# Two transformer blocks on one core: half-array products as alternating runs, rotation by VectorE across bands, second layer's modulation gathered by VectorE, first norm's modulation block by block

## The chip, the cores and the metric

The kernel runs on one core of a Trainium2 chip. TensorE (PE; its weight loads are listed as PEld) multiplies, VectorE (DVE), ScalarE (ACT) and GpSimd (POOL) work on tensors in the on-chip memory, and SyncE (SP) issues the loads. The metric is the device time of one execution in microseconds; a kernel's time is the median of several.

## The reference, cut to what matters

Two blocks follow each other on 256 tokens of width 1024, all in float32. The first has two layers; the second, which starts with a recurrence over the tokens, has one.

```python
def first_block(x, c, ctx, c_ctx, w_ada, ...):
    for l in range(2):
        mod_x = silu(c) @ w_ada[l] + b_ada[l]        # 9 vectors of 1024
        mod_c = silu(c_ctx) @ w_ada[l] + b_ada[l]
        h  = h  + 0.5 * g1  * swiglu(rms_norm(h)  * (1 + sc1)  + sh1)    # width 2816
        hc = hc + 0.5 * cg1 * swiglu(rms_norm(hc) * (1 + csc1) + csh1)
        p, pc = u @ w_in[l], uc @ w_in[l]             # u, uc: normed and modulated
        q_g, k_g = rms_norm(q_g), rms_norm(k_g)
        q_w, k_w, q_g, k_g = (rope(t, cos, sin) for t in (q_w, k_w, q_g, k_g))
        h = h + gm * (attention of three kinds @ w_out[l])
        ...                                           # hc likewise, then a second feed-forward
def _rope(x, cos, sin):                               # per head of 64
    x1, x2 = x[..., :32], x[..., 32:]
    return concatenate([x1 * cos - x2 * sin, x2 * cos + x1 * sin])
```

The second block's recurrence, per head of 64: `state = state * w + sa * b + v * k`, with `sa = state @ -kk`, and the output `state @ r`.

## The kernel before

**How it is tiled.** Channels lie on the 128 partitions in eight blocks (KB = 8), tokens along the free axis: columns 0 to 255 are x and 256 to 511 the context, so that one product of 512 columns serves both. Products of weights are in three parts: a weight tile of 1 MiB is loaded, ScalarE casts it (`whi`), VectorE forms the residue (`wlo`), both 128x1024 twice (`wtile`, L775), and each activation likewise has a cast and a residue (`split`, L813); `mm3` (L797) issues hi x hi, hi x lo and lo x hi.

**What sets the order.** The program is recorded as a list (class Plan, L388), and `schedule` (L514) lays it out by list scheduling: each engine takes the first recorded operation whose inputs are ready, with costs from `cost` (L472), within a window of 3000 operations and the memory that is free. The memory is 22 pages of 128x2048, a small area, three weight slots and eight banks. The result is one fixed order for each engine. Every instruction is emitted from one line (L739, in `emit`), so the trace knows tiles only as page, bank, small and w. `nc.run` (class Run, L374) records several products as one operation that nothing comes between.

**The modulation.** `ada_steps(l, g)` (L880) computes 2048 columns of `silu(c) @ w_ada`, for c and c_ctx at once: `cs` holds both vectors, padded to 32 columns, as the stationary side, and the loaded chunk of 128 rows x 2048 columns streams through four column groups of the array, 32 columns of the array each (`tile_position=(0, 32j)`), plain fp32. Eight chunks accumulate in a bank; `fin` (L912) turns the result around with small products and adds the bias. Group 0 of layer 0 holds the shift and scale of the first norm, and its eight chunks of 1 MiB come first in the program (`setup`, L835). The other groups are lists of steps that the feed-forward layers pop, one after each block (`pop_fill`, L819). Layer 1 is popped in `ffn(0, 2)`, the second feed-forward of layer 0: five groups, the last with 1024 columns, two chunks to a step. `pos_steps` (L1332), a table lookup on VectorE that the second block needs, is popped after it.

**The first feed-forward.** `norm` (L990) with `scaled` takes x and ctx already multiplied by their reciprocal norms and applies gain and shift; `ffn` (L1019) runs its first two blocks (`gate_up`, L1057) in halves, x's 256 columns first, and the other nine of each half with 512.

**The rotation.** In `finish` (L1150), for seven of 13 projections a layer, the projection is copied out of its bank, a product with a permutation matrix `perm` swaps the 32-row bands, and VectorE forms `t * cos + swapped * sin`.

**The half-array products.** In `rwkv_chunks` (L1632, called once for each of two groups of four heads) the products of `bt` and `kt` with `KR` use 64 rows of the array, one head; `TK` and the first part of `pY` fill 64 columns of it.

## Time and profile before

| | |
|---|---|
| time, median of 3 runs (lowest to highest) | 2390.52 us (2389.61 to 2391.29) |
| the profiled execution: time, span | 2394.02 us, 2392.2 us |
| mean granted clock of TensorE | 0.991 |
| PE, PEld, DVE, ACT, POOL busy | 2343.3, 2024.9, 1342.4, 973.4, 52.2 us |
| loaded | 325.00 MB, 136 GB/s over the span |

How to read it: the span runs from the first instruction to the last of one profiled execution, and times in the trace count from its start. "Busy" is the time in which an engine had at least one instruction under way. A product in plain fp32 shows as two records, one of the three-part kind as one.

### The profile page before, as it was taken

What the parts mean: (1) busy time and instruction counts of PE and PEld (TensorE: products, weight loads), DVE (VectorE), ACT (ScalarE), POOL (GpSimd) and SP (SyncE); (2) the same over time, 40 slices, a digit from 0 to 9 for tenths busy, and PEclk for the clock granted to TensorE, in tenths of its full rate; (3) what the DMA queues carried; (4) which work ended last, traced back from release to release, by engine and by line L of the source; (5) the groups of instructions that cost most, each with busy time, mean ns of one, the idle gap of its engine ahead of it and who ended that gap; (6) DMA issues with size and microseconds to landing.
All of it is one profiled execution on the core that took longest, in us unless ns stands there. A gap on an engine that the chain in (4) does not pass through costs nothing. (4 is left out here: it accounts for less than half of the span.)

```text
span 2392.2 us, 35707 instructions
## 1 busy us (share of the span) xinstructions
PE 2343.3 (98%) x14614; PEld 2024.9 (85%) x14614; DVE 1342.4 (56%) x2539; ACT 973.4 (41%) x1760; POOL 52.2 (2%) x64
## 2 busy tenths in 40 slices
PE   6999999999999999999999999999999999999998
PEld 4777788978787777888878889889999898999998
DVE  4322333585753597345333247866557677667874
ACT  4221223476632212233213235755456224646653
POOL 0000000000000000000000000000000000000000
PEclk8999999999999999999999999999999999999999
DMA  8646422212345573233123233134545110454543
GB/s 338 236 172 220 165 83 96 94 37 97 106 183 194 193 288 123 76 104 122 61 89 132 78 108 103 63 113 172 196 156 178 43 49 34 158 177 158 210 158 127
DMA packets 55041, 328.34 MB, mean 137 GB/s; under 512 B 7133, under 2 KB 10205, under 8 KB 24798
## 3 DMA queue, kind: packets, MB, share of 16 engines
q1 hardware_dynamic: 54878, 326.07, 38.2%
q8 instruction: 114, 1.87, 0.3%
q14 instruction: 49, 0.40, 0.0%
HBM read 325.00 MB, written 1.05 MB: 136 GB/s over the span
## 5 line engine op out<-in xcount | busy, mean ns | idle before, releaser
L739 PE MATMUL bank<-page,page 128*128 128x256 f32 (+5 forms) x13206 | 2233.9, 344 | 29.6 <-DMA page<-in_w_ada_dram 14.0
L739 PEld LDWEIGHTS bank<-page,page 128*128 128x128 f32 (+2 forms) x13206 | 1875.3, 186 | 318.6 <-issue 61.4
L739 ACT CAST page<-w 128x1024 fp32r<-128x1024 f32 (+2 forms) x511 | 488.7, 961 | 1000.0 <-PE bank L739 958.1
L739 DVE TENSOR_TENSOR page<-w,page 128x1024 fp32r<-128x1024 f32 (+2 forms) x511 | 567.5, 1113 | 541.6 <-ACT page L739 400.4
L739 DVE TENSOR_TENSOR page<-page,bank 128x512 f32<-128x512 f32 (+2 forms) x170 | 94.2, 569 | 242.9 <-PE bank L739 239.6
L739 DVE SCALAR_TENSOR_TENSOR page<-bank,small,page 128x256 f32<-128x256 f32 (+2 forms) x240 | 111.5, 484 | 98.3 <-PE bank L739 94.8
L739 PE MATMUL bank<-page 128*128 128x256 f32 (+9 forms) x564 | 141.1, 315 | 1.7 <-DVE page L739 1.6
L739 DVE TENSOR_TENSOR page<-page,page 128x256 fp32r<-128x256 f32 (+3 forms) x272 | 129.1, 490 | 15.2 <-ACT page L739 14.6
L739 ACT ACTIVATE page<-bank,small 128x256 f32<-128x256 f32 (+2 forms) x216 | 115.3, 546 | 33.4 <-DVE small L739 21.7
L739 ACT CAST page<-page 128x256 fp32r<-128x256 f32 (+1 forms) x167 | 78.2, 481 | 113.9 <-DVE page L739 111.9
L739 PEld LDWEIGHTS bank<-small,page 128*128 128x128 f32 x776 | 95.0, 167 | 25.3 <-ACT page L739 8.1
L739 ACT COPY page<-bank 128x512 f32<-128x512 f32 (+3 forms) x175 | 81.1, 497 | 85.8 <-PE bank L739 84.1
L739 PE MATMUL bank<-small,page 128*128 128x128 f32 (+4 forms) x776 | 108.2, 266 | 7.2 <-ACT page L739 4.5
L739 ACT ACTIVATE page<-bank 128x512 f32<-128x512 f32 (+3 forms) x168 | 84.2, 508 | 59.3 <-PE bank L739 58.5
L739 ACT ACTIVATE page<-page 128x256 f32<-128x256 f32 (+3 forms) x180 | 77.9, 446 | 67.1 <-DVE page L739 58.2
L739 PEld LDWEIGHTS bank<-page 128*128 128x128 f32 (+2 forms) x564 | 93.8, 190 | 9.1 <-DVE page L739 2.6
L739 DVE TENSOR_TENSOR page<-bank,page 128x256 f32<-128x256 f32 (+2 forms) x123 | 57.5, 488 | 39.8 <-PE bank L739 23.8
L739 POOL TENSOR_TENSOR small<-small 128x2 f32<-128x2 f32 (+2 forms) x32 | 38.2, 1196 | 1871.2 <-DVE small L739 1492.4
L739 DVE TENSOR_REDUCE small<-bank 128x1 f32<-128x512 f32 (+3 forms) x132 | 67.2, 526 | 3.6 <-PE bank L739 3.4
L739 ACT ACTIVATE page<-page,small 128x256 fp32r<-128x256 f32 (+1 forms) x124 | 56.9, 506 | 29.1 <-DVE page L739 28.6
L739 DVE COPY_PREDICATED page<-page,small 128x384 f32<-128x384 uint32 x124 | 64.8, 588 | 0.9
L739 DVE TENSOR_SCALAR page<-page,small 128x256 f32<-128x256 f32 (+2 forms) x136 | 53.7, 407 | 2.2 <-ACT page L739 1.1
(47 smaller groups left out, 384.9 us busy)
## 6 DMA issues: line engine op xcount, KB each, us to landing
w<-in_gu_dram SPq DMA_DIRECT2D x88, 1024.0 KB, 4.9
page<-in_w_ada_dram SPq DMA_DIRECT2D x64, 1024.0 KB, 7.4
w<-in_dn_dram SPq DMA_DIRECT2D x64, 704.0 KB, 4.1
w<-in_w_up_dram SPq DMA_DIRECT2D x22, 1024.0 KB, 4.8
w<-in_w_qk_dram SPq DMA_DIRECT2D x12, 1024.0 KB, 4.9
w<-in_w_gate_dram SPq DMA_DIRECT2D x12, 1024.0 KB, 4.9
w<-in_w_dn_dram SPq DMA_DIRECT2D x16, 704.0 KB, 4.0
page<-in_w_ada_dram SPq DMA_DIRECT2D x16, 512.0 KB, 4.6
```

The source lines that it names most:

```text
L739: getattr(getattr(self.real, eng), m_)(*a_, **k_)
```

## The change

It does five things.

- Layer 1's modulation no longer goes through TensorE chunk by chunk (`ada_steps_v`). VectorE keeps two accumulators of 128x2048, one each for c and c_ctx, and adds each chunk times its per-partition scalar (ScalarE makes the first one by a copy with a scale). At the end of a group two products per column group, with a stationary side `pick` that is all ones in one column, sum over the partitions; the ending (`ada_fin`) is the old one. A step is one chunk now, 45 steps instead of 25, and the loop that emptied the list behind `ffn(0, 2)` goes, so that what is left runs on into `ffn(1, 1)`.
- The first norm's group is laid out anew in memory (`w_ada0`): chunk k holds all 1024 rows of the shift and scale of channel block k. `first_mod` handles one chunk with eight 256-column products, two small products to turn it around, and the additions; `ffn` then scales block k of x and ctx and issues its products for the first two gate/up blocks, both halves in one, before it goes to block k + 1. The context and the small constants are loaded ahead of the chunks.
- The rotation's product goes: four operations of 32 rows read a band and write the swapped one, times a sine table whose signs are arranged for that; the cosine part and the sum follow.
- The 64-row products alternate between the two halves of the rows, in runs of four and with a bank for each half; `TK` and the first products of `pY` are runs as well.
- The planner holds back 5120 instead of 6144 columns of memory.

```diff
+    def first_mod(self, k, raw):
+        ps = self.aux_ps("ada")
+        with nc.run(cost=1100.0):
+            for i in range(2):
+                for j in range(4):
+                    b = 4 * i + j
+                    nc.tensor.matmul(ps[32 * j:32 * j + 32, :256], self.cs[:, b, :], raw[:, 256 * b:256 * b + 256],
+                                     start=i == 0, stop=i == 1, skip_group_check=True, tile_position=(0, 32 * j))
+        t = self.t("adat", [256])
+        nc.vector.tensor_copy(t, ps[:, :256])
+        pt = self.aux_ps("adaT")
+        for m in range(2):
+            nc.tensor.matmul(pt[:, 2 * m:2 * m + 2], t[:, P * m:P * m + P], self.rsum, start=True, stop=True)
...
+    def ada_steps_v(self, l, g):
...
+                for r in range(2):
+                    acc = st["acc"][r][:, :n]
+                    if k == 0:
+                        nc.scalar.activation(acc, raw[:, :n], AF.Copy, scale=self.cs[:, k, r:r + 1])
+                    else:
+                        nc.vector.scalar_tensor_tensor(acc, raw[:, :n], self.cs[:, k, r:r + 1], acc,
+                                                       op0=OP.mult, op1=OP.add)
...
+                for r in range(2):
+                    for j in range(nj):
+                        nc.tensor.matmul(ps[32 * j:32 * j + 32, :], self.pick[:, r],
+                                         st["acc"][r][:, 512 * j:512 * j + 512], start=r == 0, stop=r == 1,
+                                         skip_group_check=True, tile_position=(0, 32 * j))
...
+        elif scaled:
+            u = [self.blk(f"u{k}") for k in range(KB)]
+            first = [[self.mm_ps("pg"), self.mm_ps("pu")] for _ in range(ahead)]
+            for k in range(KB):
+                self.first_mod(k, raws[k])
...
+                for j in range(ahead):
+                    for i in range(2):
+                        self.mm3(first[j][i], w0[j], (i * KB + k) * P, u[k], both[0], k == 0, k == KB - 1)
...
-                    nc.scalar.activation(t, ps[:, :N], AF.Copy, scale=sc)
-                pr = self.aux_ps("rot")
-                nc.tensor.matmul(pr[:, :S], perm, t[:, :S], start=True, stop=True)
+                    x_ = ps
+                    if N > S:
+                        nc.scalar.activation(t[:, S:], ps[:, S:N], AF.Copy, scale=sc)
                 t1, t2 = self.t("rp1", [S]), self.t("rp2", [S])
-                nc.vector.tensor_tensor(t1, t[:, :S], cosT, op=OP.mult)
-                nc.vector.tensor_tensor(t2, pr[:, :S], sinT, op=OP.mult)
+                for r in range(0, P, 32):
+                    a_, b_ = slice(r, r + 32), slice(r ^ 32, (r ^ 32) + 32)
+                    nc.vector.scalar_tensor_tensor(t2[b_], x_[a_, :S], sc, sinT[a_], op0=OP.mult, op1=OP.mult)
+                nc.vector.scalar_tensor_tensor(t1, x_[:, :S], sc, cosT, op0=OP.mult, op1=OP.mult)
                 nc.vector.tensor_tensor(t[:, :S], t1, t2, op=OP.add)
...
         for g in range(5):
-            self.fill += self.ada_steps(1, g)
+            self.fill += self.ada_steps_v(1, g)
         self.ffn(0, 2)
-        while self.fill:
-            self.pop_fill()
...
+                pss = [self.aux_ps("pw") for _ in range(2)]
+                with nc.run(cost=2 * 450.0):
+                    for i, st in enumerate((bt, kt)):
+                        for s in range(2):
+                            hs = slice(64 * s, 64 * s + 64)
+                            nc.tensor.matmul(pss[s][:, S * i:S * i + S], st[hs, pr, P * tb:P * tb + P], KR[pr][hs, tb],
+                                             start=True, stop=True)
```

**How the order moves, at three places.** The first is the start of TensorE's order, before (32x512 are the chunks of the first modulation, 128x1 the sums of squares, 128x128 the spreading of the reciprocal norms, 128x256 from row 12 on the first feed-forward):

```order
L739 MATMUL bank0_67<-page1_78,page0_75 32x512 x4
L739 MATMUL bank0_67<-page4_86,page0_75 32x512 x4
L739 MATMUL bank1_68<-small_63,page0_75 128x1 x4
L739 MATMUL bank0_67<-page5_88,page0_75 32x512 x4
L739 MATMUL bank0_67<-page6_90,page0_75 32x512 x4
L739 MATMUL bank2_69<-small_63 128x128 x2
L739 MATMUL bank0_67<-page7_95,page0_75 32x512 x4
L739 MATMUL bank0_67<-page8_97,page0_75 32x512 x4
L739 MATMUL bank0_67<-page9_102,page0_75 32x512 x4
L739 MATMUL bank0_67<-page10_104,page0_75 32x512 x4
L739 MATMUL bank3_70<-small_63,page4_86 128x8 x4
L739 MATMUL bank4_71<-page6_198,page3_84 128x256
```

and now (32x256 are a chunk, 128x2 its small products, 128x512 the feed-forward):

```order
L740 MATMUL bank0_67<-small_63,page0_75 128x1 x4
L740 MATMUL bank1_68<-small_63 128x128 x2
L740 MATMUL bank2_69<-page4_88,page0_75 32x256 x8
L740 MATMUL bank3_70<-small_63,page0_75 128x1 x4
L740 MATMUL bank4_71<-small_63,page4_88 128x2 x2
L740 MATMUL bank5_72<-small_63 128x128 x2
L740 MATMUL bank6_73<-page5_98,page0_75 32x256 x8
L740 MATMUL bank7_74<-page6_101,page0_75 32x256 x8
L740 MATMUL bank0_67<-small_63,page16_210 128x2 x2
L740 MATMUL bank1_68<-small_63,page16_210 128x2 x2
L740 MATMUL bank3_70<-page17_229,page14_181 128x512
L740 MATMUL bank2_69<-page17_229,page14_181 128x512
```

Three chunks instead of eight stand ahead of the first product of the feed-forward, and both norms' sums instead of one norm's.

The second is VectorE's order in `ffn(0, 2)`, over two gate/up blocks, before (128x1024 are weight residues, the 128x512 that read a bank the gating products, the other 128x512 residues of their results):

```order
L739 TENSOR_TENSOR page10_256<-w2_66,page5_194 128x1024
L739 TENSOR_TENSOR page0_75<-page0_75,bank3_70 128x512
L739 TENSOR_TENSOR page17_414<-w2_66,page6_198 128x1024
L739 TENSOR_TENSOR page16_294<-page0_75,page16_294 128x512
L739 TENSOR_TENSOR page7_201<-w0_64,page8_206 128x1024
L739 TENSOR_TENSOR page0_75<-page0_75,bank2_69 128x512
L739 TENSOR_TENSOR page18_535<-w0_64,page5_194 128x1024
L739 TENSOR_TENSOR page17_414<-page0_75,page17_414 128x512
L739 TENSOR_TENSOR page10_256<-w1_65,page5_194 128x1024
L739 TENSOR_TENSOR page0_75<-page0_75,bank6_73 128x512
```

and now (the multiply-adds of the modulation are the operations of 128x2048):

```order
L740 SCALAR_TENSOR_TENSOR page14_3911<-page5_98,page0_75,page14_3911 128x2048
L740 SCALAR_TENSOR_TENSOR page16_210<-page5_98,page0_75,page16_210 128x2048
L740 TENSOR_TENSOR page4_506<-w0_64,page2_84 128x1024
L740 SCALAR_TENSOR_TENSOR page14_3911<-page10_3921,page0_75,page14_3911 128x2048
L740 TENSOR_TENSOR page0_75<-page0_75,bank4_71 128x512
L740 TENSOR_TENSOR page6_3625<-w0_64,page2_84 128x1024
L740 TENSOR_TENSOR page20_263<-page0_75,page20_263 128x512
L740 SCALAR_TENSOR_TENSOR page16_210<-page10_3921,page0_75,page16_210 128x2048
L740 SCALAR_TENSOR_TENSOR page14_3911<-page13_3960,page0_75,page14_3911 128x2048
L740 TENSOR_TENSOR page19_257<-w1_65,page6_3625 128x1024
L740 SCALAR_TENSOR_TENSOR page16_210<-page13_3960,page0_75,page16_210 128x2048
L740 TENSOR_TENSOR page0_75<-page0_75,bank6_73 128x512
```

Two or three multiply-adds of 128x2048 stand between the operations of a block, in which there was nothing but the layer's own work.

The third is TensorE's order at the 64-row products of the recurrence, before (a row of two is one head's):

```order
L739 MATMUL bank2_69<-page8_10489,page9_13239 128x256 x2
L739 MATMUL bank3_70<-page8_10489,page9_13239 128x256 x2
L739 MATMUL bank0_67<-page9_13239 128x256 x2
L739 MATMUL bank2_69<-page9_13239 128x256 x2
L739 MATMUL bank3_70<-page8_10489,page9_13239 128x256 x2
L739 MATMUL bank0_67<-page8_10489,page9_13239 128x256 x2
L739 MATMUL bank2_69<-page9_13239 128x256 x2
L739 MATMUL bank3_70<-page9_13239 128x256 x2
```

and now, for the second of the four runs of such a chunk (banks 2 and 6), with the products around it (dense ones in bank 1 and others in bank 3):

```order
L740 MATMUL bank1_68<-page13_7542,page4_7271 128x256 x2
L740 MATMUL bank1_68<-page13_7542,page5_5142 128x256
L740 MATMUL bank2_69<-page11_5865,page3_86 128x256
L740 MATMUL bank6_73<-page11_5865,page3_86 128x256
L740 MATMUL bank2_69<-page11_5865,page7_13219 128x256
L740 MATMUL bank6_73<-page11_5865,page7_13219 128x256
L740 MATMUL bank3_70<-page7_13219,page11_5865 128x64 x2
L740 MATMUL bank1_68<-page13_7542,page4_7271 128x256 x2
L740 MATMUL bank1_68<-page13_7542,page5_5142 128x256
L740 MATMUL bank1_68<-page2_84,page4_7271 128x256 x2
L740 MATMUL bank1_68<-page2_84,page5_5142 128x256
```

The heads alternate by bank, and dense products of another part stand between one run and the next.

## Rows read from the trace of the kernel before

**Rows 1.** The page's first part: engine, busy us (share of the span) x instructions

```profile
PE 2343.3 (98%) x14614; PEld 2024.9 (85%) x14614; DVE 1342.4 (56%) x2539; ACT 973.4 (41%) x1760; POOL 52.2 (2%) x64
```

**Rows 2.** Windows: us, busy (count) by engine, PEclk, DMA, GB/s; last row sums 625 to 1400

```profile
0.00:60.00 60.00, 41.39 (x264) 29.83 (x265) 28.02 (x68) 24.30 (x55) 5.69 (x16) 0.89 0.83 337
...
850.00:940.00 90.00, 90.00 (x436) 66.17 (x437) 85.24 (x159) 20.11 (x25) 0.00 (x0) 1.00 0.60 214
...
sum 775.00, PE 770.31 PEld 622.25 DVE 369.95 ACT 222.57 POOL 9.86; mean PE 110.04 PEld 88.89 DVE 52.85 ACT 31.80 POOL 1.41
```

**Rows 3.** Groups by shape, PE, whole span: busy, mean ns of one, idle before

```profile
L739 PE MATMUL bank<-page,page 128*128 128x512 f32 x4855 | 1150.0, 392 | 3.7 <-DVE page L739 3.4 <-ACT page L739 0.3
L739 PE MATMUL bank<-page,page 128*128 128x256 f32 x6371 | 844.9, 288 | 10.6 <-ACT page L739 6.9 <-DVE page L739 3.5
...
L739 PE MATMUL bank<-page,page 64*128 64x256 f32 x64 | 13.3, 397 | 0.0
...
L739 PE MATMUL bank<-small,page 128*128 128x2 f32 x72 | 8.6, 243 | 0.5 <-ACT page L739 0.5
```

**Rows 4.** Groups by shape, PE, 625 to 960 us: the 32-row products

```profile
L739 PE MATMUL bank<-page,page 128*32 128x512 f32 x288 | 35.0, 599 | 0.0
```

**Rows 5.** Timeline of the weight loads, 707 to 714: start, length, [wait before]

```profile
707.03 1.77 PEld L739 LDWEIGHTS bank<-page,page 128*128 128x128 f32 x8
...
711.02 1.01 PEld L739 LDWEIGHTS bank<-page,page 128*128 128x128 f32 x5 [0.84 <-ACT page L739]
```

**Rows 6.** Groups by shape, DVE, 625 to 1400 us

```profile
L739 DVE TENSOR_TENSOR page<-w,page 128x1024 fp32r<-128x1024 f32 x92 | 112.4, 1223 | 144.4 <-ACT page L739 119.8 <-PE bank L739 18.6 <-issue 3.5
L739 DVE COPY_PREDICATED page<-page,small 128x384 f32<-128x384 uint32 x124 | 64.8, 588 | 0.9
...
L739 DVE SCALAR_TENSOR_TENSOR page<-bank,small,page 128x256 f32<-128x256 f32 x66 | 29.1, 479 | 36.2 <-PE bank L739 36.0
L739 DVE TENSOR_TENSOR page<-page,page 128x512 fp32r<-128x512 f32 x40 | 27.5, 687 | 6.2 <-ACT page L739 6.2
```

**Rows 7.** Groups by shape, ACT, 625 to 1400 us

```profile
L739 ACT CAST page<-w 128x1024 fp32r<-128x1024 f32 x92 | 96.7, 1051 | 303.1 <-PE bank L739 303.1
...
L739 ACT CAST page<-page 128x512 fp32r<-128x512 f32 x40 | 24.8, 621 | 49.3 <-DVE page L739 49.3
```

**Rows 8.** Timeline of PE at 479 us, a rotation's product and what follows

```profile
479.53 0.60 PE L739 MATMUL bank<-page 128*128 128x256 f32 x2
479.78 2.41 PE L739 MATMUL bank<-page,page 128*128 128x512 f32 x9
```

**Rows 9.** Timeline of PE and its weight loads, 1865 to 1873: half-array products

```profile
1865.84 1.14 PE L739 MATMUL bank<-page,page 64*128 64x256 f32 x8
1866.81 1.92 PE L739 MATMUL bank<-page 64*128 64x256 f32 x7
...
1872.40 0.42 PEld L739 LDWEIGHTS bank<-small,page 128*128 128x128 f32 x4 [0.54 <-DVE page L739]
```

**Rows 10.** Timeline of PE, its loads and DVE, 0 to 75 us

```profile
10.25 3.08 DVE L739 TENSOR_TENSOR page<-page 128x256 f32<-128x256 f32 x6 [10.25 <-ACT page L739]
...
20.49 2.74 DVE L739 TENSOR_TENSOR page<-page,bank 128x256 f32<-128x256 f32 x8 [4.56 <-PE bank L739]
...
33.77 0.80 PE L739 MATMUL bank<-page,page 128*128 128x256 f32 x2 [1.48 <-ACT page L739]
...
66.93 8.26 PEld L739 LDWEIGHTS bank<-page,page 128*128 128x128 f32 x37 [0.84 <-ACT page L739]
```

**Rows 11.** Window 34 to 40 us, as rows 2

```profile
34.00:40.00 6.00, 3.71 (x16) 3.41 (x17) 6.00 (x14) 5.08 (x13) 0.00 (x0) 0.50 1.02 417
```

**Rows 12.** Timeline of DVE, 466 to 484 us

```profile
468.70 1.38 DVE L739 SCALAR_TENSOR_TENSOR page<-page,page 64x512 fp32r<-64x512 f32 x2
...
479.15 0.41 DVE L739 TENSOR_TENSOR page<-page,page 128x256 f32<-128x256 f32 x1
...
479.48 0.42 DVE L739 TENSOR_TENSOR page<-page 128x256 f32<-128x256 f32 x1
```

More of the change, by code (lines that the diff above doesn't have):

```diff
@@ L1027, in ffn, with glu @@
         ahead = 2
+        def glu(j, ps, sl):
+            m = sl.stop - sl.start
+            sg, hf = self.t("sg", [m]), self.t("hf", [m])
+            nc.scalar.activation(sg, ps[0][:, sl], AF.Silu)
+            nc.vector.tensor_tensor(hf, sg, ps[1][:, sl], op=OP.mult)
+            self.split(H[j], sl, hf)
         if one:
@@ L1047, in ffn @@
                 self.split(H[j], slice(0, S), h)
-        elif w0 is None:
+        elif scaled:
[3 more added lines that the diff above has]
+                self.first_mod(k, raws[k])
+                for r in halves:
+                    t, G, sh = scaled[r][k], self.G[l][0][:, k, r:r + 1], self.mod[l][:, k, r:r + 1]
+                    if r:
+                        nc.scalar.activation(t, t, AF.Identity, scale=G, bias=sh)
+                    else:
+                        nc.vector.tensor_scalar(t, t, G, sh, op0=OP.mult, op1=OP.add)
+                    self.split(u[k], parts[r], t)
+                for j in range(ahead):
+                    for i in range(2):
+                        self.mm3(first[j][i], w0[j], (i * KB + k) * P, u[k], both[0], k == 0, k == KB - 1)
+            for j in range(ahead):
+                glu(j, first[j], both[0])
+                self.pop_fill()
+        else:
             w0 = [self.wtile(self.a[f"gu{n}"][l, j]) for j in range(ahead)]
-        u = self.norm(l, i_n, halves, scaled, rb if one else None)
+        if not scaled:
+            u = self.norm(l, i_n, halves, rb if one else None)
         hg = self.hg[l][n - 1]
```

181 lines of the change are left out of this document (97 added, 84 removed).

## Prediction

> **What bounds the kernel now.** I read the page's first part first: TensorE is busy for 2343.3 of 2392.2 us [rows 1]. Only 49 us of the span are without a product, and the table by stages puts 18.6 of them into the first 60 us, where the products wait for data [rows 2]; from 850 to 940 us TensorE is busy 90.0 of 90 us while VectorE, too, is busy 85.2. So almost everywhere a microsecond of product that is taken off TensorE is a microsecond of time, as long as nobody becomes late; work for VectorE and ScalarE is free where they have room. The groups of products by shape give the prices [rows 3]: a 512-column product costs 1150.0 / 4855 = 0.237 us of TensorE, a 256-column one 844.9 / 6371 = 0.133 us. Their mean of 392 and 288 ns is latency, which overlaps.
>
> **Second layer's modulation.** Before, 36 groups of four 32-row products (two records each) take 35.0 us of TensorE between 625 and 960 us, 0.97 us a group [rows 4]. After, VectorE sums over the eight row blocks, and TensorE only spreads two sums per column group: 8 groups for the four full steps and one group's worth for the half one, 9 x 0.97 = 8.8 us. That is 26.2 us less. Each visit has a cost of its own besides: ordinary weight loads stop at 707.03 + 1.77 = 708.80 and resume at 711.02, 2.22 us for two groups of 0.97 [rows 5], so 0.2 to 0.3 us a visit, and 15 of 20 visits go: 3 us. I take 28 us, bounds 24 and 30.
> The sums cost VectorE 56 multiply-adds of 2048 elements and 14 of 1024. The longest there are today are additions: 1.22 us for 1024 elements, 0.69 for 512, so 1.04 ns an element and 0.15 fixed; a 256-element multiply-add (0.48, from a bank) is 0.06 above that line [rows 6]. So 2.35 and 1.28 us: 56 x 2.35 + 14 x 1.28 = 150 us. ScalarE gets eight copies of 2048 and two of 1024, on its own line of 1.05 and 0.62 us [rows 7]: 17 us, in a stage where it is the idlest.
> What hides the 150 us: from 625 to 1400 us VectorE is busy 370 of 775 [rows 2]; 520 of some 747 is 70%. The peak of before is the table lookup for the positions, 124 predicated copies, 64.8 us [rows 6]; the new order puts most of it behind the multiply-adds, into the next feed-forward layer, where there was room. The densest place of the new order is the one quoted: in four consecutive gate/up blocks VectorE has three, three, four and two multiply-adds plus the block's two weight residues, one gating product and one residue (3.8 us), about 10.9, 10.9, 12 and 9 us, against 48 products x 0.237 = 11.4 us for a block. That fits with little over, and weights are split about one block ahead. I charge 2 us for places where one multiply-add stands ahead of something wanted; bounds 0 and 10. If this cover were gone, one exposed multiply-add costs 2.35 us.
>
> **Rotation.** Fourteen matrix products of 256 columns in plain fp32 leave TensorE. One is at 479.53: its two passes end 0.60 us later, and the next product is drawn 0.25 us after it [rows 8], which are the two bounds; the half-array products of the same width take 13.3 us for 32, 0.42 each [rows 3]. I take 14 x 0.42 = 6 us, bounds 3.4 and 8.4. VectorE gets four 32-row operations for one of 128 rows, some 1.5 us more a rotation, 21 us, in stretches where it is half idle. ScalarE's copy becomes half as wide or goes.
>
> **Half-array products.** In the recurrence's preparation, 32 products use one half of the array's rows. The trace shows that halves can run together: the first four take from 1865.84 to 1866.81, 0.97 us, but all 16 of that chunk last until 1872.40, 6.56 us [rows 9], because the later ones wait for VectorE to empty a bank (0.54 us at the end, and the order shows three banks in turn). Four runs at 0.97 us would take 3.9 us, so at most 2.7 us a chunk, 5.3 for both. The new runs are apart and enter and leave the half-array mode each by itself, which costs some tenths like the visits above. The other two groups were next to each other already or gain an alternation here and there. I take 4 us, bounds 0 and 6.
>
> **First norm, block by block.** Before, the first product stands at 33.77 us, behind the eight chunks, and runs at half clock at first (the granted clock is 0.50, the lower of its levels, from 34 to 40); the first two blocks with the first four chunks of the next modulation are done when ordinary weight loads resume at 66.93 [rows 10, 11]. After, the loads are x, ctx, chunk 0, weights 0, chunks 1 and 2, weights 1, and so on; at 417 GB/s [rows 11] one of 1 MiB takes 2.5 us. But now the vector work stands first. From the first addition to the last scaled block of x took from 10.25 to 23.2 us [rows 10]; it starts 2.5 us earlier, and ahead of the first product there are also eight scalings of ctx (2.7 us), two weight residues (2.4), and the copies, additions and residues of chunk 0 (2.3): some 28 us, 6 us earlier than now. Behind it stand five chunk runs that were in front (5 us) and two small products more for each block (14 x 0.24 = 3.4 us [rows 3]); the two blocks go as 96 products of 512 columns at 0.237 instead of 192 of 256 at 0.133, 2.8 us less. 6 - 5 - 3.4 + 2.8 = 0.4: I take **nothing**, bounds 4 us lost (stays at half clock) and 6 gained.
>
> **Sum.** -28 - 6 - 4 + 0 + 2 = -36 us. The profiled execution itself took 2394.0 us (span 2392.2 and 1.8 around it), 3.5 above the median of 2390.5; its 2358.0 is 2354.5 on the scale of the medians. The other edits (a longer first constant, less memory held back by the planner, leftover steps running into the next layer) move work but add none that I could price; I count them at nothing, covered by TensorE's stream.
>
> **Rivals.** *The start pays.* If the clock is up when the products begin, because TensorE was fed from chunk 0 on, the start gives its 6 us and more than that with fewer gaps: 2347. For it: 18.6 idle us lie there. Against: VectorE's chain above. *The rotation's chain becomes the path.* A rotation took one bank operation, a product and one addition; now five operations and an addition on VectorE stand between the projection and the scores. Today like operations follow each other every 0.33 us although each lasts 0.41, but two that begin on different partitions (the 64-row pair at 468.70) take 0.69 each, with no overlap [rows 12]. So four bands cost 4 x 0.48 rather than 4 x 0.33, and if the 0.9 us by which the chain is longer were on the path each time, 14 x 0.9 = 12 us go: 2366. The Trainium skill says the same of it (VectorE: DVE Perf Modes, section "Two Vector instructions with no wait between them"): an instruction whose start quadrant differs from the last one's is held until every earlier one has finished. By that rule the bands never overlap, and the trace agrees (0.69 against 0.33 us). Against the rival: TensorE has other projections to run meanwhile. *VectorE becomes the bound of the feed-forward layer, and the kernel slower.* If of each pair of multiply-adds one comes between a weight residue or a gating product and the products waiting for it, 28 x 2.35 + 7 x 1.28 = 75 us come back, 2427; it decides from 1.3 us per pair, where the 38 us are used up, that is where VectorE's work in a block exceeds 11.4 us for more than a few blocks. For it: the four blocks above, and that the planner writes the order with shorter times than rows 6 shows. Against: 850 to 940 us of today, VectorE at 95% and TensorE without a gap.
> That the change doesn't do what it says can be for the half-array runs alone (they overlap no better than now): 2358.5, inside the forecast.
>
> **Numbers.** Forecast 0.72, the start pays 0.14, the rotation's chain 0.09, slower 0.05. Bounds of the forecast: 30 + 8.4 + 6 + 6 - 0 = 50 saved at best, 24 + 3.4 + 0 - 4 - 10 = 13 at worst, not all at once; I take 2341 to 2372, which holds the first two rivals. About 0.2% (4.8 us) is what a measurement of this kernel can tell from no change: faster 0.93, same 0.03, slower 0.04 (the slower rival and a few lucky escapes from it).
>
> **What would show it.** Right: between 625 and 1000 us no 32-row groups but five short ones, TensorE still without gaps, and VectorE near 90% there; the 32 half-array products in about 8 us instead of 13; the first product at 27 to 30 us and the first two blocks done within 4 us of 66.93 less what the two later chunks are worth; fp32 products of 256 columns gone from the attention stages. Wrong: VectorE named as what ended TensorE's idle time in the feed-forward layers, or more than 10 us of new idle time anywhere.

## The result, and the profile after

The changed kernel takes **2363.55 us** (median of 4 runs, 2361.93 to 2365.16) against 2390.15 us of the kernel before on the same chip. The ratio is 0.9884, 95% interval 0.9872 to 0.9895: 1.2% faster. On another chip it was 2363.02 against 2391.16 us, ratio 0.9879 (0.9862 to 0.9895). The forecast was 2354.5 us in a range from 2341 to 2372: right in sign, and 9 us too fast.

TensorE is still the engine that sets the time. The first part of the page of the changed kernel, which answers to [rows 1]:

```profile
PE 2309.2 (98%) x14354; PEld 2012.4 (85%) x14354; DVE 1503.5 (64%) x2676; ACT 989.3 (42%) x1763; POOL 55.8 (2%) x67
```

TensorE lost 34 us of work and VectorE gained 161. The windows of the changed kernel (columns as in [rows 2]; the second is the stretch that the forecast called the peak, the third the two feed-forward layers that share the modulation):

```profile
0.00:60.00 60.00, 45.27 (x294) 32.91 (x294) 30.35 (x91) 22.05 (x48) 7.40 (x22) 0.97 0.92 372
...
850.00:940.00 90.00, 90.00 (x415) 71.79 (x415) 82.07 (x66) 28.79 (x32) 0.00 (x0) 1.00 0.71 262
...
625.00:1400.00 775.00, 766.70 (x3722) 638.26 (x3723) 512.71 (x700) 242.65 (x350) 11.13 (x14) 0.99 0.38 136
```

In the last row VectorE is busy 513 of 775 us, where the forecast had 520. TensorE is without a product for 8.3 us there, against 4.7 before [rows 2]. Two sets of groups by shape show what replaced [rows 3, 4]: the products that spread the sums, the half-array products (the trace has 56 of their 64 records), the multiply-adds and the bands of the rotation.

```profile
L740 PE MATMUL bank<-page,small 128*32 128x512 f32 x72 | 9.6, 598 | 0.0
...
L740 PE MATMUL bank<-page,page 64*128 64x256 f32 x56 | 8.2, 395 | 0.0
```

```profile
L740 DVE SCALAR_TENSOR_TENSOR page<-page,page,page 128x2048 f32<-128x2048 f32 x56 | 130.2, 2345 | 0.1
...
L740 DVE SCALAR_TENSOR_TENSOR page<-page,page,page 128x1024 f32<-128x1024 f32 x14 | 17.7, 1280 | 0.1
L740 DVE SCALAR_TENSOR_TENSOR page<-bank,page 32x256 f32<-32x256 f32 x32 | 13.5, 420 | 1.9 <-PE bank L740 1.3
L740 DVE SCALAR_TENSOR_TENSOR page<-page,page 32x256 f32<-32x256 f32 x16 | 6.7, 417 | 0.3
```

The prices were right nearly to the digit: 2.345 and 1.280 us for a multiply-add (forecast 2.35 and 1.28), 9.6 us for the spreading products (8.8). So the missing 9 us are not in what the new work costs on its own engine. They lie in what it does to its neighbours, and in the clock.

To find the place, the span is cut at the first products of the sums of squares that open a norm (128x1 products in the timeline of TensorE); they stand in every version. Microseconds, two profiled executions of each kernel, in order of the program; the last two columns are the time for which TensorE's granted clock stood at 0.50, the lower of its two levels:

| stage | before | changed | difference of the means | forecast | lower clock, before | lower clock, changed |
|---|---|---|---|---|---|---|
| start and first feed-forward, to the first attention | 434.0, 431.3 | 429.0, 428.6 | -3.9 | 0 | 13.7, 6.8 | 3.4, 6.8 |
| first attention | 232.9, 234.5 | 235.5, 234.6 | +1.4 | -3 | 3.4, 6.8 | 6.8, 6.8 |
| two feed-forward layers with the modulation | 780.2, 779.6 | 756.2, 756.7 | -23.4 | -26 | 3.4, 3.4 | 10.2, 10.2 |
| second attention | 169.9, 169.5 | 173.2, 173.8 | +3.8 | -3 | 6.8, 6.8 | 6.8, 6.8 |
| feed-forward layer behind it | 194.4, 192.9 | 192.7, 192.7 | -0.9 | 0 | 3.4, 0 | 0, 0 |
| recurrence, up to the next norm | 378.0, 376.7 | 371.0, 371.1 | -6.3 | -4 | 6.8, 3.4 | 10.2, 10.2 |
| rest | 202.9, 203.4 | 203.6, 203.6 | +0.5 | 0 | 6.1, 8.4 | 8.9, 8.8 |

(-26 is the modulation's 28 saved less the 2 charged for waits of VectorE; the rotation's 6 is halved between the attentions.) The sum is -28.9 us between these profiled executions.

What the lower level costs can be read from the recurrence, whose work is the same in every version with the new half-array runs. It took 368.0 and 368.4 us where 3.4 us of it ran at the lower level, 369.5 to 369.7 with 6.8, and 371.0 to 371.5 with 10.2: about half a microsecond for each microsecond. With this half taken out ("at equal clock" from here on, an estimate), the differences behind the start are +0.5, -26.8, +3.8, -0.1, -8.9 and -0.4 us, and the lower clock of the changed kernel takes back some 7 us, for which the forecast had no term. (At the start, where TensorE also waits for data, the times don't follow the clock.) Differences below 1 us at equal clock say little. So neither attention is 3 us shorter, though each lost seven products of the rotation: the first is as long as before, the second longer. That is the riddle of this case.

### The profile page after: what moved, and what is told of

Same layout as the page of the kernel before. It is cut to its first block, busy times and chain, and to the rows that moved or that the text cites. A ratio compares the mean times of both kernels' runs of the same rounds, so it can differ in the third digit from the quotient of the medians.

```text
span 2361.2 us, 35354 instructions
## 1 busy us (share of the span) xinstructions
PE 2309.2 (98%) x14354; PEld 2012.4 (85%) x14354; DVE 1503.5 (64%) x2676; ACT 989.3 (42%) x1763; POOL 55.8 (2%) x67
## 5 line engine op out<-in xcount | busy, mean ns | idle before, releaser
L740 PE MATMUL bank<-page,page 128*128 128x256 f32 (+8 forms) x12812 | 2179.2, 338 | 17.0 <-ACT page L740 10.9
L740 PEld LDWEIGHTS bank<-page,page 128*128 128x128 f32 (+3 forms) x12812 | 1851.0, 187 | 279.6 <-issue 35.1
L740 PE MATMUL bank<-page 128*128 128x256 f32 (+7 forms) x610 | 149.3, 321 | 1.1 <-ACT page L740 1.1
L740 DVE SCALAR_TENSOR_TENSOR page<-page,page,page 128x2048 f32<-128x2048 f32 (+1 forms) x70 | 147.9, 2132 | 0.2
L740 DVE TENSOR_TENSOR page<-page,page 128x256 fp32r<-128x256 f32 (+4 forms) x262 | 124.3, 491 | 17.7 <-ACT page L740 17.0
L740 PEld LDWEIGHTS bank<-page 128*128 128x128 f32 (+2 forms) x610 | 99.0, 189 | 12.8 <-ACT page L740 4.6
L740 DVE TENSOR_TENSOR page<-bank,page 128x256 f32<-128x256 f32 (+2 forms) x109 | 51.7, 498 | 29.3 <-PE bank L740 14.8
```

The costliest lines, as they stand in the source:

```text
L740: getattr(getattr(self.real, eng), m_)(*a_, **k_)
```

## The experiments

All of them change one thing in the changed kernel, if nothing else is said. Times are medians, with the ratio to the kernel before on the same chip. They come from three chips (the first four experiments, the next four and the last four), and the changed kernel was timed on the second of these and, for the result, beside the kernel before; so a difference between versions of different chips is better taken from the ratios. The intervals of two versions overlap where their ratios differ by less than some 0.002, about 5 us; finer readings rest on the stages of the profiles.

### The kernel before, once more

No edit.

> The kernel before, unchanged, for a second profile, since its first one was 3.5 us above the median of the runs. Main reading: the stages repeat to within 1 us, the two attention stages take 229 us (437.9 to 666.9 us) and 150.7 us (1451.0 to 1601.7 us) again, and the 3.5 us are stretches at the lower clock in other places. Rival: a stage of the first profile was itself an outlier (the start with 13.7 us at half clock above all), then the gain of 5.8 us that the two traces show at the start shrinks to 2 or less.

Measured 2389.61 us. The feed-forward layers, both attentions (234.5 and 169.5 us by the cuts above) and the rest repeat to 1.6 us, so they can be compared. The start moved by 2.7 us (the second values of the table). The first profile's start was therefore partly an outlier, and the gain there is 2.5 to 5 us, not 6.

### What the planner holds back

```diff
-    order = plan.schedule(N_PAGES, N_SMALL, W_SLOTS, 3000, dict(m=5120, s=64))
+    order = plan.schedule(N_PAGES, N_SMALL, W_SLOTS, 3000, dict(m=6144, s=64))
```

> The changed kernel with the planner's old 6144 columns held back. Theory (the rotation on VectorE lengthens the attention stages): the time stays at 2363 +- 3, and the attention stages stay 8 us longer in sum than in the kernel before. Rival (the planner's other order under less held-back memory lengthens them, and the rotation saves the 6 us that were forecast): 2350 to 2355.

Measured 2366.78 us (ratio 0.9896, 0.9882 to 0.9911). Attentions 236.3 and 175.2 us: no shorter than in the changed kernel. The rival falls: the new order under less held-back memory is not what lengthens them. This run is the base for the other versions with 6144.

### Rotation by the product

The permutation product and its table as before, with 6144 columns held back.

```diff
-                for r in range(0, P, 32):
...
-                    nc.vector.scalar_tensor_tensor(t2[b_], x_[a_, :S], sc, sinT[a_], op0=OP.mult, op1=OP.mult)
...
+                pr = self.aux_ps("rot")
+                nc.tensor.matmul(pr[:, :S], perm, t[:, :S], start=True, stop=True)
+                nc.vector.tensor_tensor(t1, t[:, :S], cosT, op=OP.mult)
+                nc.vector.tensor_tensor(t2, pr[:, :S], sinT, op=OP.mult)
```

> The changed kernel with the rotation by the permutation product as before, and with 6144 columns held back, to be read against the run that has only the 6144. Theory (the rotation on VectorE costs more than its 14 products did): 6 to 14 us faster than that run, 2349 to 2357, the two attention stages 3 and 5 us shorter. Rival (the rotation saves the 6 us that were forecast, the loss is the order's): 6 us slower than that run.

Measured 2363.57 us (0.9885, 0.9868 to 0.9902), 3.2 us below the run before, within the noise of the two. The stages say more. The second attention fell from 175.2 to 169.7 us, the value of the kernel before: there VectorE's rotation costs time. But the first attention did not fall by 3, it rose from 236.3 to 240.8 us. That rise is the clock (13.7 us at the lower level against 3.4): at equal clock the stage takes 234.0 against 234.6 us, so the two forms cost the same there. Half of the theory holds, and the other half needs another cause.

### Half-array products as before

The old loop with one bank per head, and the two groups of 64 columns, without runs.

> The changed kernel with the half-array products in the order of before. Theory (the runs are worth the 7 us that the traces show between 1826 and 2018 us of before): 2370.5. By the forecast's term of 4 us: 2367.5. Rival (the gain of that stage comes from elsewhere): 2363.5 +- 1.5.

Measured 2367.17 us (0.9904, 0.9887 to 0.9921), 4.2 us above the changed kernel, or 4.8 to 6.0 by the ratios, since the two were timed on different chips; the recurrence takes 375.2 instead of 371.0 us. That is the forecast's 4 us, but it hides two things that nearly cancel. In this profile no part of the recurrence runs at the lower level, in the changed kernel 10.2 us do. At equal clock the recurrence takes 374.6 to 375.2 us in the three profiles with the old order and 365.9 to 366.7 in the eleven with the new one: the runs save some 9 us of TensorE's time, more than the theory's 7, and the lower clock takes back 2 to 5 of them (3.4 to 10.2 us at the lower level). All three groups of half-array products were put back at once, so the share of each is not shown.

The timeline of TensorE in the changed kernel shows two such runs next to each other, and one alone (it begins at 1847.09, inside the third row, which counts its first four records with the dense ones):

```profile
1840.79 1.57 PE L740 MATMUL bank<-page,page 64*128 64x256 f32 x12
1842.19 0.60 PE L740 MATMUL bank<-page 64*128 64x256 f32 x4
1842.72 5.08 PE L740 MATMUL bank<-page,page 128*128 128x256 f32 x37
1847.62 0.60 PE L740 MATMUL bank<-page 64*128 64x256 f32 x4
```

The first two rows are two runs, eight products, in 1.9 us (1840.79 to 1842.72), 0.97 us for four products, which in the kernel before only the first four reached; there 16 took 6.56 us in all [rows 9]. Where part of the gain is given back can be seen further on in the stage: TensorE waits 2.56 us in one piece in the changed kernel, where the run with the old order has waits of 0.89 and 0.57, and the changed kernel's clock is at 0.66 in the mean from 1984 to 1994 us. Windows of the changed kernel and, at the same place, of the run with the old order (columns as in [rows 2]):

```profile
1984.00:1994.00 10.00, 7.44 (x32) 6.51 (x31) 8.95 (x35) 3.06 (x12) 1.11 (x1) 0.66 0.00 0
```

```profile
1993.00:2003.00 10.00, 8.32 (x71) 6.53 (x71) 9.84 (x42) 6.87 (x23) 0.78 (x1) 1.00 0.01 2
```

### The changed kernel, once more

> The changed kernel itself, for its time and a second profile on the chip of the next three runs: 2363.5 +- 2; attention stage of layer 1 155.5 us, from the norm ahead of the first attention to the one behind it 235.5 us, one wait of 3.9 us behind that norm with some 10 us at the lower clock after it.

Measured 2363.02 us (0.9879, 0.9862 to 0.9895). Attentions 234.6 and 173.8 us, and the same wait of 3.88 us behind the first one.

### Multiply-adds held back behind their own layer's norm

What is in the way of the first attention? VectorE's timeline of the run with 6144 held back, in its last 15 us:

```profile
634.49 2.35 DVE L740 SCALAR_TENSOR_TENSOR page<-page,page,page 128x2048 f32<-128x2048 f32 x1
636.75 0.42 DVE L740 TENSOR_TENSOR page<-bank,page 128x256 fp32r<-128x256 f32 x1
637.08 2.35 DVE L740 SCALAR_TENSOR_TENSOR page<-page,page,page 128x2048 f32<-128x2048 f32 x1
639.34 2.44 DVE L740 SCALAR_TENSOR_TENSOR page<-bank,small,page 128x256 f32<-128x256 f32 x6
```

Multiply-adds of the modulation stand there already, and six updates of 256 columns follow one without a gap. TensorE then waits:

```profile
645.16 0.51 PE L740 MATMUL bank<-page,page 128*128 128x256 f32 x2 [1.32 <-ACT page L740]
646.48 3.69 PE L740 MATMUL bank<-page,page 128*128 128x512 f32 x15 [0.81 <-DVE page L740]
```

The steps are recorded with `ffn(0, 2)`, but the planner looks 3000 operations ahead and takes whatever is ready. So the next run makes the first one of them wait, in the plan, for the norm.

```diff
-                        nc.scalar.activation(acc, raw[:, :n], AF.Copy, scale=self.cs[:, k, r:r + 1])
+                        i = nc.scalar.activation(acc, raw[:, :n], AF.Copy, scale=self.cs[:, k, r:r + 1])
+                        if g == 0:
+                            nc.after(i, self.normed)
```

(`self.normed` is the last operation of `norm`; 6144 columns are held back.)

> The changed kernel with 6144 columns held back, and the first multiply-adds of the modulation ordered behind the norm of their own feed-forward layer. To be read against the run that has only the 6144 (2366.8). Theory (multiply-adds that VectorE takes up inside the end of the first attention, 2.35 us each, hold up its last steps): that stage falls from 236.3 to 234 us or less, its waits of 1.3 and 0.8 us at the end go, the wait behind the norm stays; 2362 to 2365. Rival (they fill gaps there and cost nothing): the same to within 1.5 us, or slower because they come later.

Measured **2356.88 us** (0.9854, 0.9839 to 0.9869), 9.9 us below the run with the 6144 alone, and 6.1 below the changed kernel. The first attention fell from 236.3 to 230.5 us, more than expected, and the feed-forward layers did not pay for it (756.8 and 756.6 us). Starting early had bought nothing. The spans of the two profiled executions differ by 5.7 us (2364.9 and 2359.2), and this stage is all of it; the rest of the 9.9 lies within the spread of the hold-back run, whose profiled execution was its slowest.

One expectation failed in an instructive way: the wait behind the norm did not stay. In the changed kernel TensorE's timeline has

```profile
667.58 0.83 PE L740 MATMUL bank<-small,page 128*128 128x1 f32 x6 [0.30 <-ACT page L740]
672.28 2.08 PE L740 MATMUL bank<-small 128*128 128x128 f32 x8 [3.88 <-POOL small L740]
```

and in the hold-back run

```profile
665.67 0.83 PE L740 MATMUL bank<-small,page 128*128 128x1 f32 x6 [0.55 <-ACT page L740]
...
667.88 0.80 PE L740 MATMUL bank<-small 128*128 128x128 f32 x2 [0.83 <-POOL small L740]
```

Between the sums (128x1) and the spreading of the reciprocal norm (128x128) stand a scaling with an addition by VectorE and a power by GpSimd, on two columns. Their timelines in the changed kernel, VectorE and then GpSimd:

```profile
666.93 2.35 DVE L740 TENSOR_TENSOR page<-w,page 128x1024 fp32r<-128x1024 f32 x2
669.20 0.22 DVE L740 TENSOR_SCALAR small<-bank 128x2 f32<-128x2 f32 x2
669.34 2.34 DVE L740 SCALAR_TENSOR_TENSOR page<-page,page,page 128x2048 f32<-128x2048 f32 x1
```

```profile
669.49 3.40 POOL L740 TENSOR_TENSOR small<-small 128x2 f32<-128x2 f32 x2 [141.53 <-DVE small L740]
```

and GpSimd's in the hold-back run:

```profile
665.27 0.70 POOL L740 TENSOR_TENSOR small<-small 128x2 f32<-128x2 f32 x1 [135.66 <-DVE small L740]
667.13 0.69 POOL L740 TENSOR_TENSOR small<-small 128x2 f32<-128x2 f32 x1 [1.17 <-PE bank L740]
```

GpSimd needs 0.70 us for a step. With a multiply-add running on VectorE from 669.34 to 671.68 the two steps take 3.40. The view of GpSimd's small tiles in the changed kernel gives the spread:

```profile
L740 POOL TENSOR_TENSOR small<-small x32: 688/1032/2736, 12.8 to 2352.1; 128x2 f32<-128x2 f32 x19, 128x4 f32<-128x4 f32 x7, 128x8 f32<-128x8 f32 x6
```

2.74 us is the longest of the 32 (the three numbers are the shortest, the median and the longest, in ns), and it is the one at 669.49. So of the wait of 3.88 us 0.8 pass before VectorE takes up the addition, behind two residues, and 2.74 are the first step, 2.04 more than it takes alone. It ends at 672.23, 0.55 us behind the multiply-add. At the same place in the kernel before, the step took 1.52 us beside a residue of 1.22 us, and ended 0.55 behind it, too; there the 32-row products stood between the sums and the spreading, and TensorE did not wait.

```profile
669.88 1.52 POOL L739 TENSOR_TENSOR small<-small 128x2 f32<-128x2 f32 x1 [137.29 <-DVE small L739]
```

The Trainium skill names the cause (SBUF — State Buffer, section "SBUF: two separate sides"): VectorE and GpSimd share a pair of ports under an exclusive lock, and a VectorE operation with two inputs from that memory, once it has started, keeps GpSimd out until it ends. The trace agrees: 0.70 us alone, 1.52 beside a residue of 1.22, 2.74 beside a multiply-add of 2.34. That page's rule bore on this change, and the forecast did not use it.

### The same, with the rotation by the product

> As the run before, and with the rotation by the permutation product. Theory (both the rotation on VectorE and the early multiply-adds cost time in the attention stages): the first attention falls from 240.8 us of the run with the product rotation alone to 233, the second stays at 150; 2354 to 2358, faster than the change. Rival (the 240.8 us have another cause): 2363.5, as with the product rotation alone.

Measured 2356.25 us (0.9848, 0.9834 to 0.9863). The first attention fell from 240.8 to 231.8 us, 6.8 of it by the clock and 2.2 at equal clock (234.0 to 231.8). So the early multiply-adds cost time with the product, too. Beside the hold-back run, the first attention is 1.3 us longer with the product (3.0 at equal clock: 231.8 against 228.8), and the second 3.2 us shorter, 170.0 against 173.2. The two nearly cancel: the rotation on VectorE is worth about nothing in sum.

### First group of the modulation through TensorE

```diff
-            self.fill += self.ada_steps_v(1, g)
+            self.fill += (self.ada_steps_v if g else self.ada_steps)(1, g)
```

> The changed kernel, with the first of the five groups of the second layer's modulation through TensorE as before, the other four on VectorE. Theory (the wait of 3.9 us behind the norm, and the 10 us at the lower clock after it, are there because the 32-row products that lay over it are gone): wait and low clock go, 7 us saved, the eight chunk runs cost 7 to 8 us, in sum 2364 +- 2. Rival (VectorE's multiply-adds and residues stand ahead of the norm's small steps): a wait of 2 us or more stays, and the time rises to 2367 to 2371.

Measured 2358.86 us (0.9862, 0.9847 to 0.9876), faster than either theory had it. The wait and the lower clock behind the norm are gone, as the theory of the missing cover said. But the first attention also fell to 232.4 us, since VectorE's multiply-adds now start later (at 714.8 instead of 621.3 us); and the hold-back run loses the wait without any 32-row product. So it was not the missing cover alone. The granted clock of the two in the 11 us around the norm, the changed kernel and then this run (columns as in [rows 2]):

```profile
668.00:679.00 11.00, 6.21 (x27) 5.53 (x27) 9.06 (x19) 6.54 (x9) 3.40 (x2) 0.57 0.72 287
```

```profile
664.00:675.00 11.00, 11.00 (x94) 8.10 (x94) 8.19 (x20) 5.09 (x11) 2.21 (x2) 1.00 0.77 302
```

TensorE was without a product for 4.8 of the 11 us in the changed kernel, and its clock lay at 0.57 in the mean, near the lower level of 0.50: the wait is paid twice.

### First norm as before

Loads, chunks, norm and the first two blocks in the old order.

> The changed kernel with the first norm's modulation and the first two blocks as before. Theory (the block-by-block start is worth what the traces show, 2.5 to 5.8 us): the first sums of squares ahead of the first attention move from 428.3 to 431 to 434 us, the time is 2365.5 to 2369. By the forecast (nothing): 2363 +- 1.5.

Measured 2365.32 us (0.9892, 0.9878 to 0.9905), 2.3 above the changed kernel and 1.9 to 3.1 by the ratios, which is within the noise; the first attention starts at 431.8 instead of 428.6 to 429.3 us in the five other profiles with 5120 columns held back. There the new start is worth 2 to 3 us, a little less than the theory's least. With 6144 it is not shown: six profiles with the new start reach the first attention at 429.3 to 431.8 us. The windows 26 to 32 and 32 to 38 us show where, in the changed kernel and then in this run:

```profile
26.00:32.00 6.00, 5.37 (x20) 4.32 (x21) 5.29 (x17) 4.73 (x10) 0.00 (x0) 0.72 1.01 418
32.00:38.00 6.00, 6.00 (x39) 4.26 (x38) 2.17 (x6) 0.78 (x2) 0.00 (x0) 1.00 1.03 405
```

```profile
26.00:32.00 6.00, 2.95 (x18) 1.94 (x16) 1.34 (x4) 1.99 (x2) 0.00 (x0) 0.75 1.01 422
32.00:38.00 6.00, 3.04 (x12) 2.75 (x13) 6.00 (x15) 4.88 (x13) 0.00 (x0) 0.50 1.03 409
```

The new start has TensorE at full clock and without a gap from 32 us on, where the old one works half of the time and at the lower level.

### Modulation of the second layer as before

> The changed kernel with the second layer's modulation through TensorE as before. Theory (its removal is worth 23.4 us between the norm behind the first attention and the one ahead of the second, and the early multiply-adds cost the first attention 4 to 6 us): that stretch rises from 756.4 to 780 us, the first attention falls from 235 to 230 us, 2381 to 2384. By the forecast's terms (28 us saved, 2 lost): 2389.

Measured 2387.84 us (0.9982, 0.9973 to 0.9991): the modulation on VectorE is worth 24.8 us (23.4 to 24.6 by the ratios) with all that it does around it, near the forecast's 26. The feed-forward layers rise to 780.0 us as the theory said and the first attention falls to 231.8 us, but the second takes 177.4, 3.6 us more than in the changed kernel, so the time lies 4 above the theory. Without the modulation the other parts of the change give 3.3 us (2391.16 less 2387.84), of which start and half-array runs alone would give 6.5. By the stages the loss lies in the second attention, 177.4 against 169.5 to 169.9 us of the kernel before, while the first is 1 to 3 us shorter than there.

### Rotation on VectorE in the first layer, product in the second

With the hold-back, and `if l == 0` around the two forms.

> As the hold-back run, with VectorE's rotation in the first layer and the product in the second. Theory (VectorE's rotation saves 3 us in the first attention, where softmax is spread over more work, and loses 3 in the second): first attention 230 us, second 166 to 170; 2353 +- 2, the fastest so far. Rival (both are the same everywhere and what differs is where the lower clock falls): 2356.5.

Measured 2357.39 us (0.9855, 0.9841 to 0.9868). The stages are as the theory says, 230.0 and 169.9 us, the better value of each; the median is not better than with either form throughout (2356.88 and 2356.25), as the rival had it, so the 3 us are not shown by the times. The profiled execution itself took 2355.7 us of span against 2359.2 of the hold-back run.

### Softmax scaling by ScalarE in the second attention

```diff
-                    nc.vector.tensor_scalar(pr, pr, rec, None, op0=OP.mult)
+                    if last:
+                        nc.scalar.activation(pr, pr, AF.Copy, scale=rec)
+                    else:
+                        nc.vector.tensor_scalar(pr, pr, rec, None, op0=OP.mult)
```

> As the hold-back run (VectorE's rotation in both layers), with the second attention's 32 scalings of the probabilities (128x512, 0.48 us each, 15 us) by ScalarE. Theory (VectorE's throughput bounds the dense softmax stretch of the second attention once the rotation stands on it): the waits of 1.4, 0.9 and 0.6 us there go, the stage falls from 173 to 169.5 us; 2353 +- 2. Rival (the rotation's chain, not the load, is what the scores wait for): the waits stay, the stage stays at 173 us or grows with ScalarE's 19 us more.

Measured 2356.06 us (0.9854, 0.984 to 0.9867). The second attention took 171.3 instead of 173.2 us, but 1.7 of this is the clock: 3.4 us of it ran at the lower level instead of 6.8, and at equal clock it took 169.6 against 169.8. In its dense stretch the waits shrank only in part. Windows of that stretch (columns as in [rows 2]): the kernel before (second profile), the changed kernel, the split rotation, and this run:

```profile
1488.00:1538.00 50.00, 49.50 (x321) 40.74 (x320) 46.51 (x134) 42.10 (x100) 3.81 (x3) 1.00 0.10 35
```

```profile
1460.00:1510.00 50.00, 45.60 (x271) 35.23 (x270) 45.67 (x127) 36.14 (x81) 4.96 (x4) 0.97 0.16 56
```

```profile
1460.00:1510.00 50.00, 49.54 (x321) 40.75 (x320) 46.28 (x134) 41.70 (x100) 4.71 (x5) 1.00 0.11 35
```

```profile
1460.00:1510.00 50.00, 46.54 (x284) 36.46 (x283) 42.26 (x118) 43.58 (x97) 4.77 (x4) 1.00 0.17 56
```

The first and third rows speak against the theory: with the product VectorE is as busy (46.5 and 46.3 of 50 us) as with its own rotation (45.7), and TensorE has hardly a gap. Taking 3.4 us off VectorE in the last row gives TensorE 0.9. VectorE's load is not what bounds this stretch; and no run moved the rotation's chain alone, so the rival isn't shown either.

## Why the prediction was right, and where it missed

The time lies in the forecast's range because its largest term was right. That the sum came within 9 us is in part luck: the rotation's term was wrong by some 6 us, the early multiply-adds cost 2 to 4 more than the charge covers, and the clock, which has no term, some 7; the half-array term was wrong by 5 and the start's by 2 to 4 the other way.

- **Second layer's modulation, 28 us saved and 2 lost to waits:** right. All in all it is worth 23 to 25 us by the run that undoes it, and 26.8 in its own stage at equal clock. The prices of the multiply-adds and the spreading products were right to 10%. One sum was wrong: a block with four multiply-adds comes to 3.8 + 4 x 2.35 = 13.2 us, not 12, above the 11.4 us of its products; the mean of the four blocks, 10.9, still fits, and no wait came of it.
- **The 2 us for waits were looked for in the wrong place.** I sought them among the blocks of the feed-forward layer, where VectorE was to be full. There TensorE has no gap in the stretch from 850 to 940 us. The cost arose ahead of that layer: the planner starts the multiply-adds inside the first attention, where they are worth 5.8 us with 6144 columns held back (236.3 to 230.5) and 2.4 to 4.0 us in the changed kernel (at equal clock 231.2 to 232.3 us in four profiles, against 228.3 to 228.8 in three with the hold-back), and one of them stands beside GpSimd's step in the norm. The order of the change has multiply-adds between the reductions and reciprocals of the attention's last softmax; I read it only at the feed-forward blocks. VectorE's timeline of the changed kernel there:

```profile
620.60 0.76 DVE L740 TENSOR_REDUCE small<-bank 128x1 f32<-128x256 f32 x2
621.27 2.34 DVE L740 SCALAR_TENSOR_TENSOR page<-page,page,page 128x2048 f32<-128x2048 f32 x1
623.53 0.42 DVE L740 TENSOR_TENSOR page<-bank,page 128x256 fp32r<-128x256 f32 x1
623.87 0.21 DVE L740 RECIPROCAL small<-small 128x1 f32<-128x1 f32 x2
```

- **Rotation, 6 us saved:** this term failed; in sum it is about nothing. The 3 us of seven products are really saved in the first attention once the multiply-adds are out of it (3.0 to 3.5 us at equal clock: 231.8 with the product, 228.3 to 228.8 with VectorE's form). In the second attention 3 to 4 us are lost instead. That the bands don't overlap was right: six in 2.60 us, 0.43 each, in the last run's timeline of VectorE:

```profile
1496.42 2.60 DVE L740 SCALAR_TENSOR_TENSOR page<-page,page 32x256 f32<-32x256 f32 x6
```

- **The rival of the rotation's chain** gave 2366 and came nearest to the time, at a chance of 0.09. Its sign for the second attention is right. Its mechanism is not shown: the waits that grew there end on ScalarE's results (1.8 us before, 5.2 after), not on VectorE's. These are the two views of TensorE's waits in the second attention, before and changed:

```profile
PE bank L739 <- ACT page L739: 1.8, 4, 0.6
PE bank L739 <- POOL small L739: 0.7, 2, 0.4
```

```profile
PE bank L740 <- ACT page L740: 5.2, 9, 1.4
PE bank L740 <- POOL small L740: 0.9, 2, 0.7
PE bank L740 <- DVE page L740: 0.5, 2, 0.3
```

- **Half-array runs, 4 us:** mis-sized, and right in the time by luck. At equal clock the runs save some 9 us, outside the bounds of 0 to 6. The forecast priced only the overlap within the 64-row products and gave the other two groups nothing; what each gave was not separated. The lower clock takes 2 to 5 us back, which leaves the 4.2.
- **First norm, nothing (4 lost to 6 gained):** mis-sized, 2 to 3 us gained. The first product of 512 columns stands at 27.74 us, inside the forecast's 27 to 30; what I left out of the sum is the clock, which is up by 32 us. That is the mechanism of the rival "the start pays", at under half its price:

```profile
27.74 2.92 PE L740 MATMUL bank<-page,page 128*128 128x512 f32 x6
```

- **VectorE as the bound, slower:** did not come about. From 850 to 940 us it is 91% busy and TensorE waits for nothing.
- **What was counted at nothing:** the 1024 columns less held back may be worth 3 to 4 us (2366.78 with the old value, 2363.02 and 2363.55 with the new), within the noise of the comparison. The lower clock costs some 7 us more behind the start than before, half of it in the two feed-forward layers: 10.2 us at the lower level instead of 3.4, all of them from 669.5 us on, beside the wait behind the norm.

The parts can't be added up to prove the account. Undone one by one they give 24.8 us (modulation), 2.3 (start) and 4.2 (half-array), 31.3 together against 28.1 measured; the some 3 us between would be the rotation's loss. The run with the old modulation gives it only as this remainder, and read by itself the loss is 3.2 us with 6144 held back and 0.6 with the hold-back, both within the noise.

**A better version.** With the multiply-adds held back the kernel takes 2356 to 2357 us whichever rotation it has, 6 to 7 us below the change (0.3%). The four versions (hold-back with VectorE's rotation, with the product, split, and with the softmax scaling on ScalarE) can't be told apart.

**Open:** why VectorE's rotation lengthens the second attention. TensorE is without a product for 8.0 to 8.7 us of that stage in eight profiles with it (10.5 in the run with the old modulation), and for 4.0 to 4.4 in the five with the product. It is not the memory held back, not the early multiply-adds (it is there with the hold-back too) and, as far as the last run tells, not VectorE's load. That the projection's bank is read longer, or that TensorE's work for the softmax stretch is used up earlier, was not tried.

## What to carry to other kernels

A bulk operation moved to an engine with room costs nothing only where nothing short and urgent stands behind it. Where a scheduler takes whatever is ready, tie the bulk work to the stage in which it is meant to run, and read the order also ahead of that stage, not only in it. And look at the other engine that shares a resource: a step of 0.70 us on GpSimd between two products became 2.74 us when VectorE began a two-input operation of 2.34 us beside it. And before a stage's time is held against a term of the forecast, look at how much of the stage ran at the lower clock in each version: here that made a gain of 9 us look like the 4 that were forecast.

## What the runs showed that was not expected

- GpSimd's small step is held for the rest of a VectorE operation. In the hold-back run the effect moves to the next norm, where two multiply-adds of 1024 elements run: the two steps take 2.86 us and TensorE waits 2.50 us for them.

```profile
1046.59 2.86 POOL L740 TENSOR_TENSOR small<-small 128x2 f32<-128x2 f32 x2 [9.18 <-DVE small L740]
```

- The runs of one version spread by up to 8 us (the hold-back run 2353.6 to 2361.2 us, the product rotation 2360.7 to 2368.9) where others stay within 1 to 6. The profiles differ mainly in how much of a stage runs at the lower clock, mostly at places with a short wait of TensorE. A profile that is 3.5 us off its median can carry most of this in a single stage, as the first one of the kernel before did at the start.
